# Mamba's step sizes laid out on 128 partitions of 160 columns instead of 32 of 544, and two durations in the schedule's model

## The chip, the core and the metric

One core of a Trainium2 chip runs the whole program in one launch. The metric is the time of one execution on the device, in microseconds (us). The core has five engines with a queue each: TensorE (PE in the profile, its weight loads apart as PEld), VectorE (DVE), ScalarE (ACT), GpSimd (POOL) and SyncE (SP), which here only issues DMAs. ACT issues a few DMAs too. An engine takes its instructions in the order of the program and waits where the next one is not ready.

## The reference

A two-layer streaming encoder over 512 prompt frames and 32 frames of a running stream, so 544 columns in the kernel. The first layer mixes with Mamba-2, the second with stick-breaking attention; both have half-step SwiGLU blocks before and after. The part that matters here, cut from the reference:

```python
zxbcdt = h @ w_in                                   # 1024 -> 5152, the last 32 are one step size per head
dt_raw = zxbcdt[..., D_INNER + CONV_DIM:]
xbc, conv_new = causal_dwconv(xbc, conv0, conv_w, conv_b)
xbc = silu(xbc)                                     # x, B and C of 4 groups of 8 heads
dt = softplus(dt_raw + dt_bias)
A = -exp(a_log)
# chunk by chunk, a = dt * A, x_c = x * dt:
a_cs = cumsum(a_c)
y_diag = einsum(C B, exp(a_cs_i - a_cs_j), x_c);  y_off = einsum(C, state) * exp(a_cs)
new_state = state * exp(a_cs[-1]) + einsum(B, exp(a_cs[-1] - a_cs), x_c)
y = (y + xs * d_skip) * silu(z);  grouped RMS norm;  out = y @ w_out
```

## The kernel before

Activations lie as 128 channels by 544 columns. A dense product is done in fp32 parts: weights and inputs are split into a high and a low part, and each 128-row chunk takes three products (high by high, high by low, low by high), each on two halves of 272 columns. The order prints them as three rows `mm<-xh,whi`, `mm<-xl,whi`, `mm<-xh,wlo`, each x2. Such three rows are called a triple below; a product of a 128-wide block of `w_in` has eight triples, and the products write two PSUM buffers (`mm`) in turn.

The Mamba stage (`mamba`, L938) cuts the 544 columns into four chunks of 128 (c = 0 to 3, the prompt) and one of 32 (c = 4, the running stream) and does the scan for four groups of eight heads, one after another (g = 0 to 3). For a chunk of a group there are

- the transposes of x (`aux<-ident,xs`) and of B (`aux<-ident,B`), and the product of C and B (`aux<-C,B`), in `turn_x`, `turn_b` and `decay`;
- the row `ab` of cumulated steps, broadcast to all partitions by an SP DMA from the DRAM copy `acs_d` (`load_ab`, L1139). There are two buffers `ab`, so a chunk's load waits for the output block of the chunk two before;
- on ACT the distances (`ex<-ab,tok`, 8 instructions), their exponential and that of `ab`; on DVE `ex<-ex,cb`; on POOL `ab<-ab,C` and the old state by its decay, `st<-st,fade`;
- the state product (`aux<-xw,btok`), and the output block (`output`, L1267): per pair of heads `aux<-ex,xd`, and for c > 0 `aux<-ab,st`. A block of c > 0 has 16 matmuls in the order, 8 for c = 0. Here it is called the output block of the chunk.

Step sizes come first (`steps`, L961). One dense block `dt` (unit 40 of `win`) gives 32 useful rows; its other 96 rows repeat other columns and are not read. On 32 partitions by 544 columns DVE does some twenty instructions for the softplus, then the scan `acs`; ACT writes `acs` to DRAM and makes `wend`; then, for each of the five chunks, PE transposes `acs`, `dt` and `wend` and DVE copies them to `tok`.

Between these pieces PE does the stage's dense products (`dense`), in the order of MSEQ (L40): inputs of a group (B, C, four x blocks), gates (z), outputs (o). Inputs go through `conv` (DVE, ACT, POOL), and a product waits for a free `mm` buffer, which its conv or gate frees, and for its split weights (`whi` by ACT or POOL, `wlo` by DVE).

The order on PE, DVE, ACT and POOL is not written out. `Plan` (L56) holds a model: each chain of work is a generator that yields steps `("T", duration, emit)` and the like ("T" is PE, "V" and "W" DVE, "S" ACT, "G" POOL), waits and slots. `Plan.run` (L137) always takes the step that can start first in the model, the lower rank on a tie, calls its emit, and moves the model's clock on by the duration given. The emitted order is then kept on the chip (`ordered`, L1396). So a duration in a `yield` changes the order of everything behind it, and nothing else. The dense chain has rank 50, after all others, and fills PE in the model.

Of the kernel before, what the change touches and what calls it, by code (L numbers as in the profile page):

```python
# [4 lines left out]
F32 = mybir.dt.float32  # L5
F32R = mybir.dt.float32r
BF16 = mybir.dt.bfloat16
AF = mybir.ActivationFunctionType
ALU = mybir.AluOpType

P = 128
# [159 lines left out]
def s_cost(n, psum=False):  # L171
    return n / 1200.0 + (0.052 if psum else 0.094)


def v_cost(n):
    return n / 960.0 + 0.069


def _body(tc, io):
# [22 lines left out]
    with ExitStack() as ctx:  # L202
# [3 lines left out]
        def halves(ap):  # L206
            return ap.rearrange("p (a b) -> p a b", a=2)
# [47 lines left out]
        convb = vecs[:, 96:120]  # L255
        ssmg = vecs[:, 120:136]
        dskip = vecs[:, 136:152]
        dtb = vecs[0:32, 152:153]
        alog = vecs[0:32, 153:154]
        hist = const.tile([P, 24, 3], F32, name="hist")  # L260
        nc.sync.dma_start(hist, io["hist"])

# [675 lines left out]
        def mamba(norm, after, ready, ahead):  # L938
            with tc.tile_pool(name="mt", bufs=1, reuse_waits="tile") as tmp, \
# [11 lines left out]
                chunks = [(c * P, P) for c in range(NCH)] + [(TP, TS)]  # L951
                tok = tmp.tile([P, 5, 96], F32, tag="tok", name="tok")
                cstate = tmp.tile([P, 24, 6], F32, tag="cstate", name="cstate")
                acs_d = pd.tile([32, T], F32, name="acs_d")
                acoef = const.tile([32, 1], F32, name="acoef")
                got = {}

                def hm(name, tag, bufs):
                    return tmp.tile([32, T], F32, tag=tag, name=name, bufs=bufs)

                def steps(ps):  # L961

                    cost = v_cost(T)
                    yield "wait", "r"
                    rv = halves(norm.r[:, :])
                    v = hm("dv", "ex", 2)
                    yield "W", cost, lambda: V.tensor_tensor(out=halves(v[:, :]), in0=ps[0:32, :, :H], in1=rv[0:32], op=ALU.mult)
                    yield "put", "mm"
                    yield "S", 0.15, lambda: S.activation(acoef, alog, AF.Exp), "exp"
                    yield "V", 0.08, lambda: V.tensor_scalar(acoef, acoef, -1.0, None, op0=ALU.mult)  # L970
                    yield "V", cost, lambda: V.tensor_scalar(v, v, dtb, None, op0=ALU.add)
                    e = hm("de", "ex", 2)
                    yield "V", cost, lambda: V.scalar_tensor_tensor(out=e, in0=v, scalar=-1.0, in1=v, op0=ALU.mult, op1=ALU.min)
                    yield "S", s_cost(T), lambda: S.activation(e, e, AF.Exp), "exp"
                    s = hm("ds", "xd", 2)
                    yield "V", cost, lambda: V.tensor_scalar(s, e, 2.0, None, op0=ALU.add)
                    yield "V", 3.5, lambda: V.reciprocal(s, s)
                    yield "V", cost, lambda: V.tensor_tensor(out=s, in0=s, in1=e, op=ALU.mult)
                    s2 = hm("dw", "xd", 2)
                    yield "V", cost, lambda: V.tensor_tensor(out=s2, in0=s, in1=s, op=ALU.mult)  # L980
                    q = hm("dq", "xw", 2)
                    yield "V", cost, lambda: V.tensor_scalar(q, s2, 1.0 / 17.0, None, op0=ALU.mult)
                    for k in (15, 13, 11, 9, 7, 5, 3):
                        yield "V", cost, lambda: V.scalar_tensor_tensor(out=q, in0=q, scalar=1.0 / k, in1=s2, op0=ALU.add, op1=ALU.mult)
                    yield "V", cost, lambda: V.scalar_tensor_tensor(out=q, in0=q, scalar=1.0, in1=s, op0=ALU.add, op1=ALU.mult)
                    yield "V", cost, lambda: V.tensor_scalar(q, q, 2.0, None, op0=ALU.mult)
                    dtt = hm("dt", "st", 3)
                    yield "V", cost, lambda: V.scalar_tensor_tensor(out=dtt, in0=v, scalar=0.0, in1=q, op0=ALU.max, op1=ALU.add)
                    a = hm("da", "xw", 2)
                    yield "V", cost, lambda: V.tensor_scalar(a, dtt, acoef, None, op0=ALU.mult)  # L990
                    keep = hm("keep", "ab", 2)

                    def starts():
                        G.memset(keep, 1.0)
                        for c in range(5):
                            G.memset(keep[:, c * P:c * P + 1], 0.0)
                    yield "G", 1.0, starts
                    acs = hm("acs", "st", 3)
                    yield "V", 2 * cost, lambda: V.tensor_tensor_scan(acs, keep, a, 0.0, ALU.mult, ALU.add)
                    nc.scalar.dma_start(acs_d, acs)  # L1000
                    wend = hm("wend", "st", 3)

                    def ends():
                        for o, n in chunks:
                            S.activation(wend[:, o:o + n], acs[:, o:o + n], AF.Exp, scale=-1.0, bias=acs[:, o + n - 1:o + n])
                    yield "S", 5 * s_cost(P), ends, "exp"
                    for c, (o, n) in enumerate(chunks):
                        yield "get", "aux"
                        pt = aux()

                        def turn():
                            for j, src in enumerate((acs, dtt, wend)):
                                TE.transpose(pt[:n, j * 32:(j + 1) * 32], src[:, o:o + n], ident[:32, :32])
                        yield "T", 0.3, turn
                        yield "W", v_cost(96), lambda: V.tensor_copy(tok[:n, c, :], pt[:n, 0:96])
                        yield "put", "aux"
                    yield "set", "tok"

                def scale():
# [119 lines left out]
                def load_ab(g, c):  # L1139
                    off, n = chunks[c]  # L1140
                    yield "wait", "tok", ("in", g, 4)
                    if g > 0:
                        yield "wait", ("ab", g - 1, 4)
                    yield "get", "ab"
                    ab = got["ab", g, c] = tmp.tile([P, 8, n], F32, tag="ab", name="ab", bufs=2)
                    nc.sync.dma_start(ab, acs_d[8 * g:8 * g + 8, off:off + n].partition_broadcast(P))
                    yield "sleep", 5.0
                    yield "set", ("ab", g, c)

# [117 lines left out]
                def output(g, c):  # L1267
                    off, n = chunks[c]
                    src = off if c < 4 else SOFF
                    xs = got["x", g]  # L1270
                    need = [("ex", g, c), ("xd", g, c), ("xw", g, c), ("cd", g, c)]
                    yield "wait", *need
                    if c > 0:
                        yield "wait", ("st", g, before(c))
                    if c == 0:
                        yield "get", "y"
                        got["y", g] = tmp.tile([P, 4, T], F32, tag="y", name="y", bufs=NY)
                        yield "set", ("y0", g)
                    else:
                        yield "wait", ("y0", g)  # L1280
                    yield "get", "aux"
                    py = aux()
                    xd, ex, ab = got["xd", g, c], got["ex", g, c], got["ab", g, c]

                    def emit(t):
                        for b in range(2):
                            h = 2 * t + b
                            dst = py[64 * b:64 * b + 64, t * P:t * P + n]
                            TE.matmul(dst, xd[:n, h, :], ex[:n, h, :], start=True, stop=c == 0)
                            if c > 0:  # L1290
                                TE.matmul(dst, got["st", g, before(c)][:, h, :], ab[:, h, :], start=False, stop=True)
                    for t in range(4):
                        yield "T", (0.24 if n < P else 0.52) if c else 0.25, lambda: emit(t)
                    yield "set", ("y", g, c)
                    yield "put", "ex"
                    yield "put", "xd"
                    yield "put", "ab"
                    pyv = py[:, :].rearrange("p (t i) -> p t i", t=4)[:, :, :n]
                    yv = got["y", g][:, :, off:off + n]

                    def skip(t):
                        V.scalar_tensor_tensor(out=yv[:, t], in0=xs[:, t, src:src + n], scalar=dskip[:, 4 * g + t:4 * g + t + 1], in1=pyv[:, t],
                                               op0=ALU.mult, op1=ALU.add)
                    for t in range(4):
                        yield "W", v_cost(n) + 0.06, lambda: skip(t)
                    yield "put", "aux"
                    yield "set", ("out", g, c)
# [789 lines left out]
```

## Time and profile before

| | |
|---|---|
| median of 3 runs | 2349.7 us (2348.56 to 2353.23) |
| the profiled execution | 2348.45 us |
| its span in the profile | 2346.7 us |
| PE busy | 2307.8 us, 98% |
| DVE busy | 1714.5 us, 73% |
| ACT busy | 1048.6 us, 45% |
| POOL busy | 592.2 us, 25% |
| mean granted TensorE clock | 0.988 of full |

The page counts an engine as busy while one of its instructions runs, so PE at 98% says how little it waits, not how fast it is: the clock that was granted stands apart (1.00 is 2.4 GHz, 0.50 is 1.2 GHz). Times in a row of the timeline are from the start of the span; what stands in brackets at its end is how long the engine sat idle before it, and what ended that.

### The profile page before, as it was taken

The numbers are of one execution on the slowest core, as the hardware profiler recorded it, in microseconds if no ns is written. First come the engines' busy times: TensorE is split into PE (matmuls) and PEld (weight loads), VectorE is DVE, ScalarE is ACT, GpSimd is POOL, SyncE is SP. The second block draws the span as 40 slices with busy tenths as digits, with TensorE's granted clock in tenths as the row PEclk, the third lists the DMA queues.
The fourth block names the chain that finished last, engine by engine and source line by source line (L and its number), as shares of the span: only waits on it lengthen the run. The fifth ranks groups of instructions, "written<-read, shape, count | busy, mean of one in ns | idle before, by whom it ended". The sixth has DMA issues, their size and how long they took to land.

```text
span 2346.7 us, 42561 instructions
## 1 busy us (share of the span) xinstructions
PE 2307.8 (98%) x17759; PEld 2216.6 (94%) x17766; DVE 1714.5 (73%) x2236; ACT 1048.6 (45%) x1530; POOL 592.2 (25%) x575
## 2 busy tenths in 40 slices
PE   9999999989999999999999999999999999999997
PEld 8999999979999999999999999999965799999997
DVE  7677786777877676777857767777678686777857
ACT  5333334477646353333345433333478553333343
POOL 3322122144323022221211122211333122122214
PEclk9999999999999999999999999999998999999999
DMA  5233323333333232333233333232211132333232
GB/s 158 78 104 104 95 67 91 106 89 102 100 101 88 82 118 78 103 104 95 66 106 94 115 100 91 90 108 67 87 41 32 37 117 74 107 91 104 64 104 75
DMA packets 112081, 213.17 MB, mean 91 GB/s; under 512 B 12528, under 2 KB 34544, under 8 KB 111888
## 3 DMA queue, kind: packets, MB, share of 16 engines
q1 hardware_dynamic: 109104, 204.92, 29.6%
q10 hardware_dynamic: 2784, 5.52, 0.7%
q8 instruction: 140, 2.29, 0.4%
q14 instruction: 53, 0.43, 0.1%
HBM read 204.83 MB, written 5.58 MB: 90 GB/s over the span
## 4 chain that ended last, share of the span: by engine, by line
PE 92%; DVE 4%; ACT 2%; DMA 1%; issue 1%; POOL 0%; SPq 0%; DVEq 0%; ACTq 0%; POOLq 0%
PE mm L191 81%; PE z L191 5%; PE aux L191 4%; PE f L191 1%; PE o L191 1%; DVE wlo L191 1%; DVE xl L191 1%; ACT whi L191 1%; DVE x L191 1%; DMA x<-in_x 0%; DMA wraw<-in_wpg 0%; DVE fu L191 0%; DVE sl L191 0%; ACT zt L191 0%; POOL ab L191 0%
## 5 line engine op out<-in xcount | busy, mean ns | idle before, releaser
L191 PE MATMUL mm<-xh,whi 128*128 128x272 f32 x2096 | 514.3, 293 | 1.1 <-ACT whi L191 0.5
L191 PE MATMUL mm<-xl,whi 128*128 128x272 f32 x2096 | 509.9, 291 | 2.5 <-DVE xl L191 2.5
L191 PE MATMUL mm<-xh,wlo 128*128 128x272 f32 x2096 | 508.4, 291 | 2.1 <-DVE wlo L191 2.1
L191 ACT ACTIVATE whi<-wraw 128x1024 fp32r<-128x1024 f32 (+3 forms) x220 | 189.1, 860 | 409.2 <-PE mm L191 284.3
L191 PEld LDWEIGHTS mm<-xh,whi 128*128 128x128 f32 x2096 | 360.1, 190 | 9.9 <-issue 7.8
L191 PEld LDWEIGHTS mm<-xh,wlo 128*128 128x128 f32 x2096 | 360.3, 190 | 2.9 <-DVE wlo L191 2.9
L191 PEld LDWEIGHTS mm<-xl,whi 128*128 128x128 f32 x2096 | 359.7, 190 | 3.6 <-DVE xl L191 3.5
L191 PE MATMUL mm<-xfh,whi 128*128 128x272 f32 x1152 | 332.0, 288 | 0.0
L191 PE MATMUL mm<-xfl,whi 128*128 128x272 f32 x1152 | 331.9, 288 | 0.0
L191 PE MATMUL mm<-xfh,wlo 128*128 128x272 f32 x1152 | 331.7, 288 | 0.0
L191 DVE TENSOR_TENSOR wlo<-wraw,whi 128x1024 fp32r<-128x1024 f32 (+3 forms) x253 | 257.5, 1018 | 71.1 <-ACT whi L191 56.1
L191 PE MATMUL mm<-hh,whi 128*128 128x272 f32 x1408 | 291.3, 288 | 0.0
L191 PE MATMUL mm<-hh,wlo 128*128 128x272 f32 x1408 | 291.0, 288 | 0.0
L191 PE MATMUL mm<-hl,whi 128*128 128x272 f32 x1408 | 290.7, 288 | 0.0
L191 ACT ACTIVATE whi<-a 128x1024 fp32r<-128x1024 f32 x126 | 133.8, 1062 | 311.0 <-PE mm L191 202.8
L191 DVE TENSOR_TENSOR wlo<-a,whi 128x1024 fp32r<-128x1024 f32 x144 | 176.5, 1225 | 102.2 <-ACT whi L191 68.9
L191 PEld LDWEIGHTS mm<-hl,whi 128*128 128x128 f32 x1408 | 221.2, 188 | 0.0
L191 PEld LDWEIGHTS mm<-hh,whi 128*128 128x128 f32 x1408 | 220.9, 188 | 0.0
L191 PEld LDWEIGHTS mm<-hh,wlo 128*128 128x128 f32 x1408 | 220.4, 188 | 0.2 <-DVE wlo L191 0.2
L191 PEld LDWEIGHTS mm<-xfh,wlo 128*128 128x128 f32 x1152 | 216.8, 188 | 0.0
L191 PEld LDWEIGHTS mm<-xfl,whi 128*128 128x128 f32 x1152 | 216.8, 188 | 0.0
L191 PEld LDWEIGHTS mm<-xfh,whi 128*128 128x128 f32 x1152 | 216.7, 188 | 0.0
(291 smaller groups left out, 4223.4 us busy)
## 6 DMA issues: line engine op xcount, KB each, us to landing
a<-in_wgu SPq DMA_DIRECT2D x144, 512.0 KB, 4.0
wraw<-in_wd SPq DMA_DIRECT2D x128, 256.0 KB, 2.7
wraw<-in_win SPq DMA_DIRECT2D x41, 512.0 KB, 3.7
wraw<-in_wgu SPq DMA_DIRECT2D x30, 512.0 KB, 3.6
wraw<-in_wd SPq DMA_DIRECT2D x32, 384.0 KB, 3.2
ab<-acs_d SPq DMA_DIRECT2D x16, 512.0 KB, 4.8
wraw<-in_wout SPq DMA_DIRECT2D x16, 512.0 KB, 3.7
wraw<-in_wpg SPq DMA_DIRECT2D x16, 512.0 KB, 3.6
```

The costliest lines, as they stand in the source:

```text
L191: ins = getattr(self.engine, op)(*args, **kw)
```

## The change

Five edits, all in the Mamba stage and its host-side layout:

- Unit 40 of `win` repeats the 32 step columns four times, so the product `dt` gives the same 32 rows on all four quarters of the partitions. Its shape stays.
- `steps` takes from quarter c the columns of chunk c, and from the first quarter chunk 4, in six DVE instructions, so the chain works on 128 partitions by 160 columns. Bias and `a_log` are repeated alike.
- `acs`, `dt` and `wend` are turned by three transposes of 128 by 128 and three of 32 by 32 in one piece instead of five pieces of three, and two DVE copies fill `tok` instead of five.
- `acs_d` has 128 rows of 160, and `load_ab` reads its eight rows from quarter c.
- In the model, one fourth of an output block is now 0.87 instead of 0.52 (c = 1 to 3), 1.2 instead of 0.24 (c = 4) and 0.44 instead of 0.25 (c = 0). The model's durations of the step chain follow its new shapes.

```diff
-        dtb = vecs[0:32, 152:153]
-        alog = vecs[0:32, 153:154]
+        dtb = vecs[:, 152:153]
+        alog = vecs[:, 153:154]
...
-                acs_d = pd.tile([32, T], F32, name="acs_d")
-                acoef = const.tile([32, 1], F32, name="acoef")
+                acs_d = pd.tile([P, P + TS], F32, name="acs_d")
+                acoef = const.tile([P, 1], F32, name="acoef")
...
-                    return tmp.tile([32, T], F32, tag=tag, name=name, bufs=bufs)
+                    return tmp.tile([P, P + TS], F32, tag=tag, name=name, bufs=bufs)
...
-                    rv = halves(norm.r[:, :])
                     v = hm("dv", "ex", 2)
-                    yield "W", cost, lambda: V.tensor_tensor(out=halves(v[:, :]), in0=ps[0:32, :, :H], in1=rv[0:32], op=ALU.mult)
+
+                    def pieces():
+                        V.memset(v[:, P:], 0.0)
+                        for c, (o, n) in enumerate(chunks):
+                            rows = slice(32 * (c % 4), 32 * (c % 4) + 32)
+                            at = 0 if c < 4 else P
+                            while n:
+                                a, b = divmod(o, H)
+                                m = min(n, H - b)
+                                V.tensor_tensor(out=v[rows, at:at + m], in0=ps[rows, a, b:b + m], in1=norm.r[rows, o:o + m], op=ALU.mult)
+                                o, n, at = o + m, n - m, at + m
+                    yield "W", 0.1 + 5 * v_cost(P) + 0.1, pieces
...
-                    yield "V", 3.5, lambda: V.reciprocal(s, s)
+                    yield "V", 1.1, lambda: V.reciprocal(s, s)
...
-                        for c in range(5):
-                            G.memset(keep[:, c * P:c * P + 1], 0.0)
-                    yield "G", 1.0, starts
+                        for c in (0, P):
+                            G.memset(keep[:, c:c + 1], 0.0)
+                    yield "G", 0.4, starts
...
-                        for o, n in chunks:
+                        for o, n in ((0, P), (P, TS)):
                             S.activation(wend[:, o:o + n], acs[:, o:o + n], AF.Exp, scale=-1.0, bias=acs[:, o + n - 1:o + n])
-                    yield "S", 5 * s_cost(P), ends, "exp"
-                    for c, (o, n) in enumerate(chunks):
-                        yield "get", "aux"
-                        pt = aux()
-
-                        def turn():
-                            for j, src in enumerate((acs, dtt, wend)):
-                                TE.transpose(pt[:n, j * 32:(j + 1) * 32], src[:, o:o + n], ident[:32, :32])
-                        yield "T", 0.3, turn
-                        yield "W", v_cost(96), lambda: V.tensor_copy(tok[:n, c, :], pt[:n, 0:96])
-                        yield "put", "aux"
+                    yield "S", 2 * s_cost(P), ends, "exp"
+                    yield "get", "aux"
+                    pt = aux()
+
+                    def turn():
+                        for j, src in enumerate((acs, dtt, wend)):
+                            TE.transpose(pt[:, j * P:(j + 1) * P], src[:, :P], ident)
+                            TE.transpose(pt[:TS, 384 + j * 32:416 + j * 32], src[:32, P:], ident[:32, :32])
+                    yield "T", 0.6, turn
+
+                    def turned():
+                        V.tensor_copy(tok[:, 0:4, :].rearrange("p c (j h) -> p c j h", j=3), pt[:, 0:384].rearrange("p (j c h) -> p c j h", j=3, c=4))
+                        V.tensor_copy(tok[:TS, 4, :], pt[:TS, 384:480])
+                    yield "W", v_cost(384) + v_cost(96), turned
+                    yield "put", "aux"
...
-                    nc.sync.dma_start(ab, acs_d[8 * g:8 * g + 8, off:off + n].partition_broadcast(P))
+                    rows, at = (32 * c + 8 * g, 0) if c < 4 else (8 * g, P)
+                    nc.sync.dma_start(ab, acs_d[rows:rows + 8, at:at + n].partition_broadcast(P))
...
-                        yield "T", (0.24 if n < P else 0.52) if c else 0.25, lambda: emit(t)
+                        yield "T", (1.2 if n < P else 0.87) if c else 0.44, lambda: emit(t)
...
-    col = np.zeros((P, 2), np.float32)
-    col[:32, 0] = g["ssm_dt_bias"][0]
-    col[:32, 1] = g["ssm_a_log"][0]
+    col = np.tile(np.stack([g["ssm_dt_bias"][0], g["ssm_a_log"][0]], axis=1), (4, 1))
...
-    a["win"] = np.concatenate([units(win[:, :5120]), units(np.concatenate([win[:, 5120:], win[:, 5024:5120]], axis=1))], axis=0)
+    a["win"] = np.concatenate([units(win[:, :5120]), units(np.tile(win[:, 5120:], (1, 4)))], axis=0)
```

What PE does around the turning of the step sizes, before (the first of five such pieces and the start of the second; `acs`, `dt`, `wend` are the step chain's results):

```order
L191 MATMUL aux<-ident,acs 128x32
L191 MATMUL aux<-ident,dt 128x32
L191 MATMUL aux<-ident,wend 128x32
L191 MATMUL mm<-xh_4016,whi 128x272 x2
L191 MATMUL mm<-xl_4017,whi 128x272 x2
L191 MATMUL mm<-xh_4016,wlo 128x272 x2
L191 MATMUL mm<-xh_4047,whi 128x272 x2
L191 MATMUL mm<-xl_4048,whi 128x272 x2
L191 MATMUL mm<-xh_4047,wlo 128x272 x2
L191 MATMUL aux<-ident,acs 128x32
```

And in the change, where the whole turning is one piece:

```order
L191 MATMUL aux<-ident,acs 128x128
L191 MATMUL aux<-ident,acs 32x32
L191 MATMUL aux<-ident,dt 128x128
L191 MATMUL aux<-ident,dt 32x32
L191 MATMUL aux<-ident,wend 128x128
L191 MATMUL aux<-ident,wend 32x32
L191 MATMUL mm<-xh_4289,whi 128x272 x2
```

Between the norm's product at the start of the stage (`aux<-acc,ones`) and the first turning stand 83 triples before and 65 in the change, so the scan of the first group begins 18 triples earlier.

PE in the first group's scan, from the last matmul of the output block of chunk 2 to the first of chunk 3, before:

```order
L191 MATMUL aux<-ab,st 64x128
L191 MATMUL aux<-xw,btok 128x512
L191 MATMUL aux<-ident,xs 32x128 x4
L191 MATMUL aux<-ident,B 32x128
L191 MATMUL aux<-C,B 32x32
L191 MATMUL aux<-ex,xd 64x128
```

And in the change, from the same matmul on:

```order
L191 MATMUL aux<-ab,st 64x128
L191 MATMUL aux<-xw,btok 128x512
L191 MATMUL mm<-xh_4189,whi 128x272 x2
L191 MATMUL mm<-xl_4190,whi 128x272 x2
L191 MATMUL mm<-xh_4189,wlo 128x272 x2
L191 MATMUL mm<-xh_4240,whi 128x272 x2
L191 MATMUL mm<-xl_4241,whi 128x272 x2
L191 MATMUL mm<-xh_4240,wlo 128x272 x2
L191 MATMUL aux<-ident,xs 32x128 x4
L191 MATMUL aux<-ident,B 32x128
```

After these stand two more triples, `aux<-C,B`, two triples, and then the output block of chunk 3. Before, no triple stands between the output blocks of chunks 2, 3 and 4 of the first group; now six and two do (and between chunks 1 and 2 five, where two stood).

PE at the border of the second and the third group, before: the end of the second group's output block of chunk 4, behind which 18 triples come ahead of the next scan piece.

```order
L191 MATMUL aux<-ex,xd 64x32
L191 MATMUL aux<-ab,st 64x32
L191 MATMUL mm<-xh_4329,whi 128x272 x2
L191 MATMUL mm<-xl_4330,whi 128x272 x2
L191 MATMUL mm<-xh_4329,wlo 128x272 x2
```

In the change the third group's first output block (`aux<-ex,xd 64x128 x8`) follows two triples behind it:

```order
L191 MATMUL aux<-ab,st 64x32
L191 MATMUL aux<-xw,btok 128x512
L191 MATMUL mm<-xh_4289,whi 128x272 x2
L191 MATMUL mm<-xl_4290,whi 128x272 x2
L191 MATMUL mm<-xh_4289,wlo 128x272 x2
L191 MATMUL aux<-ident,xs 128x128 x4
L191 MATMUL aux<-ident,B 128x128
L191 MATMUL mm<-xh_4329,whi 128x272 x2
L191 MATMUL mm<-xl_4330,whi 128x272 x2
L191 MATMUL mm<-xh_4329,wlo 128x272 x2
L191 MATMUL aux<-ex,xd 64x128 x8
L191 MATMUL aux<-C,B 128x128
```

On ACT the same place reads, in the change (`out_ssm_s<-st` writes the second group's last state out; `ex`, `ab` behind it are the third group's chunk 0):

```order
L191 ACTIVATE ex<-ex 32x256
L191 ACTIVATE ab<-ab 128x256
L1277 DMA out_ssm_s<-st 128x512
L191 ACTIVATE ex<-ab,tok 128x128 x8
L191 ACTIVATE ex<-ex 128x1024
L191 ACTIVATE ab<-ab 128x1024
```

Before, convolution work of the third group stands behind that DMA, and the third group's distances come later.

The triples between output blocks in the four groups (from the end of one to the start of the next, c = 0 to 1, 1 to 2, 2 to 3, 3 to 4) are, before: 20, 2, 0, 0; 8, 14, 6, 7; 18, 9, 4, 7; 17, 9, 5, 18. In the change: 15, 5, 6, 2; 13, 8, 2, 6; 16, 6, 4, 12; 19, 4, 18, 0.

## Rows read from the trace of the kernel before

**Rows 1.** The page, part 1: busy us, share of the span, instructions.

```profile
PE 2307.8 (98%) x17759; PEld 2216.6 (94%) x17766; DVE 1714.5 (73%) x2236; ACT 1048.6 (45%) x1530; POOL 592.2 (25%) x575
```

**Rows 2.** Windows: length, busy by engine, granted clock (third last), DMA share, GB/s.

```profile
391.00:840.00 449.00, 440.36 (x3526) 416.17 (x3525) 334.14 (x567) 253.44 (x408) 139.77 (x174) 0.97 0.34 97
501.71:523.40 21.69, 13.05 (x91) 9.23 (x89) 16.19 (x35) 14.73 (x28) 12.40 (x12) 0.76 0.23 68
506.40:509.82 3.42, 3.42 (x24) 2.58 (x21) 2.82 (x6) 1.02 (x2) 1.90 (x3) 0.50 0.00 0
513.23:520.06 6.83, 3.55 (x30) 3.18 (x31) 2.96 (x7) 5.46 (x13) 4.34 (x3) 0.50 0.06 22
...
584.91:588.32 3.41, 3.41 (x17) 3.41 (x16) 2.73 (x6) 1.33 (x2) 0.00 (x0) 0.50 0.76 169
```

**Rows 3.** Timeline of PE, first group's chunks 2 to 4: start, duration, [idle before].

```profile
503.38 0.49 PE L191 MATMUL aux<-C,B 128*128 128x128 f32 x2 [1.40 <-DVE xd L191]
...
505.73 0.32 PE L191 MATMUL aux<-ab,st 128*64 128x128 f32 x1 [1.50 <-POOL ab L191]
...
515.35 0.66 PE L191 MATMUL aux<-ex,xd 128*64 128x128 f32 x2 [4.24 <-DVE xd L191]
517.17 0.48 PE L191 MATMUL aux<-ab,st 128*64 128x128 f32 x1 [1.16 <-POOL ab L191]
...
523.04 0.27 PE L191 MATMUL aux<-ex,xd 32*64 32x32 f32 x2 [0.35 <-DVE xd L191]
```

**Rows 4.** Timeline of ACT in the same stretch: what it waited for.

```profile
508.28 0.66 ACT L191 ACTIVATE xs<-cv 128x547 f32<-128x547 f32 x1 [1.52 <-DVE cv L191]
```

**Rows 5.** Timeline of PE: starts of pairs of rows that give a pitch.

```profile
454.29 0.41 PE L191 MATMUL mm<-xh,wlo 128*128 128x272 f32 x2
...
455.29 0.41 PE L191 MATMUL mm<-xl,whi 128*128 128x272 f32 x2
...
461.92 0.41 PE L191 MATMUL mm<-xh,wlo 128*128 128x272 f32 x2
...
463.20 0.42 PE L191 MATMUL mm<-xl,whi 128*128 128x272 f32 x2
...
466.82 0.41 PE L191 MATMUL mm<-xh,whi 128*128 128x272 f32 x2
...
469.83 0.41 PE L191 MATMUL mm<-xh,whi 128*128 128x272 f32 x2
...
496.86 0.45 PE L191 MATMUL aux<-ex,xd 128*64 128x128 f32 x4
...
498.81 1.13 PE L191 MATMUL aux<-xw,btok 128*128 128x512 f32 x2
...
500.02 0.41 PE L191 MATMUL mm<-xl,whi 128*128 128x272 f32 x2
...
580.16 0.30 PE L191 MATMUL aux<-ex,xd 32*64 32x32 f32 x2
...
583.59 0.30 PE L191 MATMUL aux<-ab,st 128*64 128x32 f32 x2
```

**Rows 6.** Timeline of SP, POOL and PE, third group: chunk 3 behind chunk 1.

```profile
632.88 0.38 SPq L1146 DMA_DIRECT2D ab<-acs_d  x1
644.29 2.36 POOL L191 TENSOR_TENSOR ab<-ab,C 128x1024 f32<-128x1024 f32 x1 [1.70 <-DVE fade L191]
648.25 0.45 PE L191 MATMUL aux<-ex,xd 128*64 128x128 f32 x4
```

**Rows 7.** Timeline of DVE: the step chain.

```profile
411.23 3.53 DVE L191 RECIPROCAL ds<-ds 32x544 f32<-32x544 f32 x1
...
446.73 0.71 DVE L191 SCALAR_TENSOR_TENSOR dt<-dv,dq 32x544 f32<-32x544 f32 x1
```

**Rows 8.** Timeline of POOL, first group: one operation at two places.

```profile
463.58 1.04 POOL L191 TENSOR_TENSOR xw<-xd,tok 128x512 f32<-128x512 f32 x1 [19.23 <-DVE xd L191]
...
494.85 2.04 POOL L191 TENSOR_TENSOR xw<-xd,tok 128x512 f32<-128x512 f32 x1
```

More of the change, by code (lines that the diff above doesn't have):

```diff
@@ L953, in mamba @@
                 cstate = tmp.tile([P, 24, 6], F32, tag="cstate", name="cstate")
-                acs_d = pd.tile([32, T], F32, name="acs_d")
-                acoef = const.tile([32, 1], F32, name="acoef")
+                acs_d = pd.tile([P, P + TS], F32, name="acs_d")
+                acoef = const.tile([P, 1], F32, name="acoef")
                 got = {}
                 def hm(name, tag, bufs):
-                    return tmp.tile([32, T], F32, tag=tag, name=name, bufs=bufs)
+                    return tmp.tile([P, P + TS], F32, tag=tag, name=name, bufs=bufs)
                 def steps(ps):
-                    cost = v_cost(T)
+                    cost = v_cost(P + TS)
                     yield "wait", "r"
-                    rv = halves(norm.r[:, :])
                     v = hm("dv", "ex", 2)
-                    yield "W", cost, lambda: V.tensor_tensor(out=halves(v[:, :]), in0=ps[0:32, :, :H], in1=rv[0:32], op=ALU.mult)
+                    def pieces():
[9 more added lines that the diff above has]
+                    yield "W", 0.1 + 5 * v_cost(P) + 0.1, pieces
                     yield "put", "mm"
@@ L973, in steps @@
                     yield "V", cost, lambda: V.scalar_tensor_tensor(out=e, in0=v, scalar=-1.0, in1=v, op0=ALU.mult, op1=ALU.min)
-                    yield "S", s_cost(T), lambda: S.activation(e, e, AF.Exp), "exp"
+                    yield "S", s_cost(P + TS), lambda: S.activation(e, e, AF.Exp), "exp"
                     s = hm("ds", "xd", 2)
                     yield "V", cost, lambda: V.tensor_scalar(s, e, 2.0, None, op0=ALU.add)
-                    yield "V", 3.5, lambda: V.reciprocal(s, s)
+                    yield "V", 1.1, lambda: V.reciprocal(s, s)
                     yield "V", cost, lambda: V.tensor_tensor(out=s, in0=s, in1=e, op=ALU.mult)
```

## Prediction

> **What bounds the kernel now.** I read the page's busy times first: PE is busy 2307.8 us of the span [rows 1], so only what PE does, waits for, or does at a lower clock counts, and other engines matter where they make it wait. Then the windows, with the Mamba stage apart: 449.00 us with PE busy 440.36, so 8.64 us idle, at a mean granted clock of 0.97 [rows 2]. A second window shows where: 501.71 to 523.40 has 21.69 us with PE busy 13.05, again 8.64. All the idle time of the stage lies in the first group's chunks 2, 3 and 4. The timeline of PE there gives five waits: 1.40 on DVE's xd, 1.50 on POOL's ab, 4.24 and 1.16 on the same two a chunk later, and 0.35 [rows 3], together 8.65.
>
> Why PE waits there is read from the order and from ACT. Between these output blocks PE has two, none and none triples to do, so it stands as soon as a chunk's inputs are late. They are late because `ab` and `ex` go through ACT, and ACT stood 1.52 us for a convolution that DVE had not finished [rows 4]: the convolutions of the second group share the engines with the scan, and no dense product comes, since both `mm` buffers wait for just these convolutions.
>
> The clock: it is granted at 0.50 (1.2 GHz) in two stretches of that place, one with PE busy 3.42 us, one with 3.55 [rows 2]. Before them PE had waited. There is another kind: at 584.91 the clock falls for 3.41 us though PE is busy throughout, right behind the output block of chunk 4 that ends at 583.59 with its small matmuls [rows 2, 5]. The windows show this one; the stage has four, one behind each group's chunk 4.
>
> **The change part by part.**
>
> *The step chain.* Twelve DVE instructions like the one of 0.71 us [rows 7] and five cheaper ones go from 544 to 160 columns, the reciprocal of 3.53 by the same ratio to some 1.0; six short ones and a memset replace the first multiplication. I estimate 17 us of DVE before and 8 after. PE waits for nothing of this now: all idle time of the stage is elsewhere [rows 2, 3]. So I cost it at nothing. Its cover is the dense products ahead of the turning, 65 triples of 0.753 us (four take 3.01, rows 466.82 and 469.83 [rows 5]). The change draws on that cover: the turning stands 18 triples, 13.6 us, earlier. If the chain is late there, PE waits for `wend`; its last parts (scan, table load, two exponentials) I put some 0.8 us ahead of PE. From a loss of 1 us to nothing; I take nothing, because DVE gets lighter.
>
> *The turning.* From 454.29 to 455.29 is 1.00 us for two rows that take 0.50 at the pitch above, so three narrow transposes cost 0.50; five such pieces 2.5. The new piece has six. The nearest rows are the four wide transposes, one of B and one product: 461.92 to 463.20 less 0.50, so 0.78 [rows 5]. I take 0.8: a gain of 1.7; from 1.0 to 2.0.
>
> *The first group's scan.* Now 15, 5, 6 and 2 triples stand between its output blocks. Is that enough? The longest chain is from the end of a block, which frees `ab`, to the block two chunks on: load, distances, two exponentials, POOL's product. In the third group of the trace it runs from 632.88 to 644.29 + 2.36 = 646.65, so 13.8 us, and PE starts that block at 648.25 [rows 6] without a wait. In the change, PE has between the end of chunk 1's block and chunk 3's: 11 triples (8.3), one block (496.86 to 498.81, so 1.95 [rows 5]), two state products (at most 1.13 each, the row at 498.81; I take 0.9) and transposes of 1.3: 13.4 us. So chunk 3 comes about 0.4 us late, and I add 0.5 for each of chunks 2 and 4. The 8.65 us of waits goes, 1.4 comes: and with the long waits the two low stretches that follow them, worth half of 3.42 + 3.55, so 3.5 us. The four stretches behind chunk 4 I leave as they are.
>
> The Trainium skill, in "TensorE: Matmul & The Clock Gate" under "HAM oscillation", says that the clock falls when TensorE has stood idle too long between bursts. By that rule the stretches behind chunk 4 would not exist, and a schedule without idle time would gain their 4 x 1.7 us too. The row at 584.91 shows a fall with PE busy for all of it, so the trace does not agree, and the sum leaves that out.
>
> *The other groups.* The model now holds a block of c > 0 at 4 x 0.87 = 3.48 us, and it takes 1.95; chunk 4 at 4.8, and it takes 3.66 (580.16 to 583.59 and the last row's 0.30 [rows 5]); before it held 2.08 and 0.96. So where the model was too quick for PE it is now too slow: PE reaches the next piece earlier than planned, by 1.5 us for each wide block, and waits for inputs that were ordered just in time. The counted triples show it. Second group, chunk 1 to 3: 10 triples, a block, two state products, transposes, 12.6 us against 13.8, so 1.2 of wait; chunk 4, 8 triples between, 1 us (nothing at best, 2.8 if its chain is as long as chunk 3's). Border to the third group: only two triples lie between chunk 4's block and the next group's first, and on ACT that group's distances stand behind the output DMA of the old state. From the DMA on, distances, exponential and DVE's product follow one another, and behind that `xd` and POOL's `xw` for the next state product. I put 1 us of wait on the block and 1 on the state product. Third group, chunk 1 to 3, with 10 triples and a norm's product: 13.1 against 13.8, so 0.7. Fourth: 0.5, since 18 triples stand ahead of chunk 3. Together 5.4, and with the border a further low stretch, 1.7.
>
> POOL decides how far this is right: `xw` takes 1.04 us at one place and 2.04 at another, beside DVE's work [rows 8]. With the longer value in each of these six chains the waits grow by 6 us; with the shorter and slack elsewhere they can vanish. The Trainium skill explains it, in "SBUF — State Buffer" under "Who interferes with whom": the two engines share a port pair that one of them holds for a whole instruction. The trace agrees (2.04 for 1.04); by the page alone no wait can be placed.
>
> *The rest.* `acs_d` is written once and read in the same amounts; the loads keep their size. Six instructions in place of one hold the `dt` buffer some 1 us longer at the stage's start; the next product into it stands about 1 us behind. Nothing, up to 0.5 lost.
>
> **The sum**, against the profiled execution of 2348.45 us: 8.65 + 3.5 + 1.7 = 13.85 gained; 1.4 + 5.4 + 1.7 = 8.5 given back; 5.4 less, so 2343.1. The median of the runs is 2349.7, 1.25 above that execution; half of this I put on: 2343.6 us.
>
> **Rivals.**
>
> 1. *The scan is simply filled.* The new waits stay at 2 us and no low stretch is added: 13.85 - 2 = 11.9 less, 2337.5. For it: three of four groups run without a wait now with as few as 4 to 9 triples between blocks. Against: these had a model that made PE late, not early.
>
> 2. *The stall moves.* First group filled, but what PE gains there it stands elsewhere: waits of 10 and two more stretches (3.4) cancel the 13.85: 2348.5 to 2350. For it: the lead of 1.5 us a block is systematic, the gain is one place.
>
> 3. *The model leads PE too far.* Twelve wide blocks at 1.5 us and four of chunk 4 at 1.1 make 22.6 us of waits if no slack takes any up, and with waits in each of three groups three more low stretches come, 5.1. Then 13.85 - 27.7, so 14 us slower, 2362. It decides from the point where all that is new passes 13.85; at a middling 20 it is 2355. Against: the model's triple is 0.705 us (`t_cost`) and takes 0.753, which gives back 13 us over the 273 triples between the first output block and the last, and much dense work stands at most places.
>
> 4. *The change does not do what it says*: the durations are called measured, and 0.87 is not what the row of 1.95 for four gives. That is the ground of 2 and 3 and has no chance of its own.
>
> **How the numbers follow.** The forecast (about 3 to 9 us less) 0.47, rival 1 0.22, rival 2 0.20, rival 3 0.11. A measurement of this kernel can tell about 0.2% from no change, 4.7 us. Rival 1 and three quarters of the forecast lie below 2345.0, so faster 0.57; the rest of the forecast and most of rival 2 within, 0.31; rival 3 and a little of 2 above 2354.4, 0.12. The range takes in the forecast and rivals 1 and 2: 2336 to 2352. The likeliest case by itself is 2340 to 2347.
>
> **What would show it.** Right: in the first group's scan no wait of PE over 1 us, and the clock at 1.00 until chunk 4's block has ended; one low stretch still behind most chunk 4 blocks; small waits before output blocks and state products of the second and third groups, the largest at their border; the stage some 5 us shorter. The step chain's DVE rows near 0.3 us. Wrong: the first group still waits several us at chunk 2 or 3; a wait for `wend` at the turning; waits of over 10 us in groups two to four; or low stretches scattered over the stage with PE busy.

## The result, and the profile after

The changed kernel takes 2337.44 us (median of 4 runs, 2335.02 to 2337.85), the kernel before 2349.13 beside it: ratio 0.995, interval 0.9938 to 0.9963, 11.7 us faster. The forecast was 2343.6, with a range of 2336 to 2352. So sign and range held, and the gain was twice the forecast; the experiments show that one of the change's two halves made a larger gain, and that the other half took a part of it away.

The page of the change, part 1 (answers to [rows 1]; the profiled execution took 2335.02 us, its span 2332.9):

```profile
PE 2295.5 (98%) x17750; PEld 2206.8 (95%) x17757; DVE 1707.0 (73%) x2237; ACT 1045.5 (45%) x1528; POOL 599.3 (26%) x570
```

I compare the stage between the start of its first and of its last norm product (`aux<-acc,ones`), which leaves out dense work at its ends that has no wait. Windows of the kernel before: length, busy by engine, granted clock third last.

```profile
391.10:793.59 402.49, 393.85 (x3156) 369.70 (x3155) 299.02 (x524) 232.03 (x378) 129.23 (x167) 0.97 0.34 97
```

The same of the change, with the stretches at half clock, and (585.10) the second group's block of chunk 4 for contrast:

```profile
389.43:783.85 394.42, 389.82 (x3147) 366.52 (x3146) 290.86 (x525) 229.16 (x376) 134.63 (x162) 0.98 0.34 99
498.04:501.46 3.42, 3.42 (x18) 3.42 (x17) 2.27 (x6) 2.35 (x4) 0.00 (x0) 0.50 0.52 158
585.10:588.50 3.40, 3.40 (x31) 2.82 (x30) 1.09 (x3) 1.60 (x6) 1.60 (x2) 1.00 0.22 82
641.40:644.82 3.42, 3.42 (x17) 3.24 (x17) 1.42 (x5) 0.00 (x0) 0.00 (x0) 0.50 0.43 132
750.63:757.46 6.83, 6.83 (x34) 6.57 (x33) 3.56 (x9) 1.32 (x2) 0.00 (x0) 0.50 0.10 38
```

The stage is 8.07 us shorter. Half of that is idle time: 402.49 - 393.85 = 8.64 before, 394.42 - 389.82 = 4.60 now. The other half, 4.03, is PE's busy time, at 0.50 for 13.67 us now where it was for 23.91 before, 20.63 of them with PE busy (six windows; three of them in [rows 2]).

All waits of PE in the stage, in the timeline (start, duration, idle before and who ended it); compare [rows 3]:

```profile
489.83 0.69 PE L191 MATMUL aux<-xw,btok 32*128 32x512 f32 x1 [0.90 <-POOL xw L191]
...
493.75 0.24 PE L191 MATMUL aux<-ab,st 128*64 128x32 f32 x1 [0.86 <-POOL ab L191]
...
592.60 0.33 PE L191 MATMUL aux<-ex,xd 128*64 128x128 f32 x2 [0.64 <-DVE y L191]
...
594.62 0.70 PE L191 MATMUL aux<-xw,btok 128*128 128x512 f32 x1 [0.51 <-POOL xw L191]
...
615.56 0.35 PE L191 MATMUL aux<-C,B 128*128 128x128 f32 x1 [0.46 <-DVE fade L191]
...
629.53 0.66 PE L191 MATMUL aux<-xw,btok 32*128 32x512 f32 x1 [0.80 <-DVE btok L191]
...
748.11 0.30 PE L191 MATMUL aux<-ab,st 128*64 128x32 f32 x2 [0.30 <-POOL ab L191]
```

Two stand in the first group, two at the border to the third, two in the third, one in the fourth: no wait over 1 us, 4.47 together.

The turning, in PE's timeline, and on ACT the exponentials that it needs:

```profile
438.51 0.62 ACT L191 ACTIVATE wend<-acs 128x128 f32<-128x128 f32 x2
```

```profile
439.32 0.40 PE L191 MATMUL aux<-ident,acs 128*128 128x128 f32 x2
439.66 0.46 PE L191 MATMUL aux<-ident,dt 128*128 128x128 f32 x2
440.05 0.46 PE L191 MATMUL aux<-ident,wend 128*128 128x128 f32 x2
440.44 0.52 PE L191 MATMUL mm<-xh,whi 128*128 128x272 f32 x2
```

`wend` is there at 439.13, 0.9 us ahead of its transpose, and six transposes take 1.12 us. The step chain on DVE (answers to [rows 7]):

```profile
408.41 1.15 DVE L191 RECIPROCAL ds<-ds 128x160 f32<-128x160 f32 x1
...
428.18 0.32 DVE L191 SCALAR_TENSOR_TENSOR dt<-dv,dq 128x160 f32<-128x160 f32 x1
```

Outside the stage 5.7 us of the profiles' difference of 13.8 remain: 1.7 ahead of it, and 4.0 in the attention stage (1667.05 to 1907.29 before), where PE runs the same instructions in the same order:

```profile
1667.05:1907.29 240.24, 230.69 (x1293) 169.38 (x1299) 180.96 (x279) 158.69 (x274) 75.48 (x83) 0.97 0.19 57
```

```profile
1657.36:1893.56 236.20, 225.84 (x1294) 166.18 (x1299) 181.12 (x279) 158.53 (x274) 75.84 (x83) 1.00 0.19 58
```

The idle time there is 9.55 before and 10.36 after; what differs is the clock (0.97, 1.00).

### The profile page after: what moved, and what is told of

It reads as the page before. It is cut to its first block, busy times and chain, and to the rows that moved or that the text cites. A ratio compares the mean times of both kernels' runs of the same rounds, so it can differ in the third digit from the quotient of the medians.

```text
span 2332.9 us, 42534 instructions
## 1 busy us (share of the span) xinstructions
PE 2295.5 (98%) x17750; PEld 2206.8 (95%) x17757; DVE 1707.0 (73%) x2237; ACT 1045.5 (45%) x1528; POOL 599.3 (26%) x570
## 4 chain that ended last, share of the span: by engine, by line
PE 89%; DVE 5%; ACT 2%; issue 2%; POOL 1%; DMA 1%; SPq 0%; DVEq 0%; ACTq 0%; POOLq 0%
PE mm L191 80%; PE z L191 5%; PE aux L191 2%; PE f L191 1%; DVE wlo L191 1%; PE o L191 1%; POOL ab L191 1%; DVE xl L191 1%; ACT whi L191 1%; DVE x L191 1%; DMA x<-in_x 0%; DVE sl L191 0%; DMA wraw<-in_wpg 0%; DVE fu L191 0%; POOL st L191 0%
```

## The experiments

The question was which half of the change, the layout or the durations, made the gain, and by what. Theory A: the scan's place in the plan, which follows from the length that the planner gives the step chain. Theory B: the durations, or the work saved.

All results in one table. "Stage" is the window above, "idle" its length less PE's busy time, "low" the time in it at a granted clock of 0.50, each of the profiled execution.

| kernel | median us (runs) | ratio to before, interval | stage | idle | low |
|---|---|---|---|---|---|
| before, first profile | 2349.13 (4) | | 402.49 | 8.64 | 23.9 |
| before, second profile | 2356.13 (1) | | 411.91 | 9.12 | 44.4 |
| the change | 2337.44 (4) | 0.9938 to 0.9963 | 394.42 | 4.60 | 13.7 |
| the change again | 2338.11 (5) | 0.9939 to 0.9965 | 394.45 | 4.66 | 13.7 |
| durations alone | 2355.57 (11) | 1.0013 to 1.0031 | 413.38 | 10.31 | 44.4 |
| layout alone | 2330.49 (6) | 0.991 to 0.9936 | 386.89 | 0.90 | 6.8 |
| layout alone again | 2332.10 (6) | 0.9904 to 0.9933 | 386.86 | 0.90 | 6.8 |
| layout, measured durations | 2341.99 (5) | 0.9953 to 0.9977 | 396.52 | 5.07 | 20.5 |
| layout, chunk 4's duration | 2336.12 (5) | 0.9927 to 0.9955 | 391.66 | 2.76 | 13.6 |
| layout, wide blocks' duration | 2340.44 (5) | 0.9946 to 0.9976 | 395.21 | 3.54 | 20.5 |
| layout, near durations | 2334.40 (5) | 0.9916 to 0.9944 | 390.36 | 0.87 | 13.7 |
| layout, shorter durations | 2339.36 (5) | 0.9937 to 0.9966 | 398.26 | 4.18 | 23.9 |
| layout, old chain costs | 2348.05 (11) | 0.9982 to 1.0 | 399.68 | 5.88 | 27.3 |
| before, short chain costs | 2338.84 (6) | 0.9934 to 0.9962 | 392.61 | 3.55 | 10.2 |

**Durations alone.** The kernel before with all three durations of the change:

```
-  yield "T", (0.24 if n < P else 0.52) if c else 0.25, lambda: emit(t)
+  yield "T", (1.2 if n < P else 0.87) if c else 0.44, lambda: emit(t)
```

> The kernel before with only the three durations of the output block changed (1.2, 0.87 and 0.44); the step sizes stay on 32 partitions. In its order the first group's output blocks have 20, 2, 0 and 0 triples between them, as before. Theory A (the moved turning and the lighter step chain fill the first group's scan, the durations only redistribute triples among the later groups and cost small waits there): the five waits of 8.65 us stay, some 0 to 5 us of new waits come in groups two to four; 2348 to 2354 us. Theory B (the durations fill the scan): the first group's waits shrink to under 3 us and the time falls to 2340 to 2343 us.

Slower, by 0.13 to 0.31%: theory A, a little above its range. The first group keeps its waits (PE's timeline, two of them), PE's idle time is 1.2 to 1.7 us more than in the two profiles of the kernel before, and a long stretch at half clock follows (windows):

```profile
512.46 0.40 PE L191 MATMUL aux<-ex,xd 128*64 128x128 f32 x2 [4.26 <-DVE xd L191]
514.27 0.48 PE L191 MATMUL aux<-ab,st 128*64 128x128 f32 x1 [1.42 <-POOL ab L191]
```

```profile
389.14:802.52 413.38, 403.07 (x3156) 376.66 (x3155) 297.01 (x522) 238.49 (x385) 140.91 (x165) 0.95 0.34 94
513.11:533.59 20.48, 18.84 (x90) 14.46 (x91) 8.51 (x21) 10.05 (x25) 6.25 (x7) 0.50 0.27 78
```

The kernel before has such a long stretch in its second profile too (below), so it need not come from the durations. What makes up the rest of the 6.6 us between the medians is not shown.

**Layout alone.** The changed kernel with the line above set back to 0.24, 0.52 and 0.25.

> The changed kernel with the old durations of the output block (0.24, 0.52 and 0.25): the layout alone. In its order the first group's output blocks have 22, 7, 17 and 2 triples between them, groups two to four 20, 8, 13, 8; 16, 6, 7, 12; 17, 9, 5, 18. Theory A: the first group runs with less than 2 us of waits and the later groups wait for nothing or little, because more triples stand between the blocks than in the change; 2334 to 2338 us, as fast as the change or up to 3 us faster. Theory B (the durations make the gain): the waits of the first group are still over 5 us and the time is 2344 to 2349 us.

2330.49, faster than A expected, and 7.6 less than the change beside it on the same chip (2338.11). The stage in windows, with the only stretch at half clock:

```profile
389.54:776.43 386.89, 385.99 (x3148) 363.25 (x3147) 291.98 (x527) 232.62 (x377) 123.94 (x163) 0.99 0.35 101
645.24:652.06 6.82, 6.82 (x34) 6.50 (x33) 4.15 (x9) 0.66 (x1) 0.00 (x0) 0.50 0.30 93
```

Against the change the stage is 7.53 us shorter: 3.70 idle and 3.83 busy, and half of the 6.85 us of low clock that is gone is 3.4. So the layout makes the whole gain, and the durations cost on either layout. This version beats both kernels.

**Layout with measured durations.** `(0.91 if n < P else 0.49) if c else 0.27`.

> The changed kernel with the durations that the trace gives for an output block: a quarter of 1.95 us (0.49), of 3.66 us (0.91) and for the first chunk 0.27. Triples between the blocks: 18, 6, 10, 7; 26, 8, 8, 4; 14, 11, 5, 2; 17, 9, 5, 9. Theory A: within 2 us of the layout alone, 2334 to 2338 us, since the first group is filled in both and the later groups keep 4 triples or more nearly everywhere. A rival, that long durations are what helps because they keep PE from being late: between the change and the kernel before, 2339 to 2345 us.

Theory A missed: 2341.99, slower than the change. One wait makes most of the idle time, in PE's timeline and on DVE, which frees the `mm` buffer:

```profile
580.57 0.49 PE L191 MATMUL mm<-xh,whi 128*128 128x272 f32 x2 [3.76 <-DVE zt L191]
```

```profile
579.72 0.70 DVE L191 TENSOR_TENSOR zt<-mm,r 128x544 f32<-128x544 f32 x1
```

No output block waits there: in the new order `zt` stands on DVE behind `wlo` and the scan's `xd`, `btok` and `cb`. Truer numbers did not make a better plan.

**Which duration costs.** Chunk 4's alone (`(1.2 if n < P else 0.52) if c else 0.25`) and the wide blocks' alone (`(0.24 if n < P else 0.87) if c else 0.44`):

> The changed kernel with the old duration for the wide blocks (0.52 and 0.25) and the new one for chunk 4 (1.2). Triples between the blocks: 22, 7, 17, 2; 23, 12, 6, 8; 12, 6, 15, 5; 17, 9, 5, 18. Theory A1: the first group waits for nothing, the others for under 1 us, 2329 to 2333 us. Theory A2: 2336 to 2340 us.

> The changed kernel with the old duration for chunk 4 alone (0.24 in place of 1.2); the wide blocks stay at 0.87 and 0.44. Triples between the blocks: 15, 5, 6, 2; 11, 9, 6, 9; 20, 7, 4, 1; 19, 4, 18, 0. Theory A1 (the wide blocks' duration of 0.87 gives back what the layout gains): the first group waits some 1.8 us as in the change, 2336 to 2340 us. Theory A2 (chunk 4's duration of 1.2 does it, by the border of the second and third groups): 2330 to 2333 us.

2336.12 and 2340.44: each costs without the other, so A1 and A2 both fail as explanations of the whole. The layout alone did not run on this chip; the kernel before took 2349.64 on it, and 2349.01 beside the layout alone (2330.49), so for chunk 4's duration, whose interval overlaps with that of the layout alone, the cost is the less certain one. The two costs do not add up to that of both, 7.6. With chunk 4's alone the largest wait, 1.99 us, is again one that the triples between blocks did not show, for ACT's `xs`:

```profile
517.78 0.48 PE L191 MATMUL aux<-ident,xs 128*128 128x128 f32 x1 [1.99 <-ACT xs L191]
```

**Layout with near, and with shorter durations.** `(0.24 if n < P else 0.49) if c else 0.27` and `(0.24 if n < P else 0.2) if c else 0.1`:

> The layout alone with the wide block's durations set to the measured ones and chunk 4's kept at 0.24: 0.49 for 0.52 and 0.27 for 0.25, a change of some 0.1 us for a block. Triples between the blocks: 18, 6, 10, 7; 28, 14, 12, 2; 16, 6, 17, 7; 17, 9, 5, 9. If the accuracy of these numbers is what matters, it is at most 1 us from the layout alone, 2329 to 2332 us. If the plan turns on small differences (three of four groups get another order), a wait of several us can come from another place, as the 3.76 us for an `mm` buffer with the measured durations: 2334 to 2343 us.

> The layout alone with durations of the output block below the measured ones (0.2, chunk 4 0.24, first chunk 0.1). Triples between the blocks: 22, 10, 11, 5; 17, 14, 14, 9; 14, 10, 8, 18; 24, 12, 11, 4: nowhere under 4, where the layout alone has a 2 in the first group. If the number of triples between blocks decides, this is as fast as the layout alone or up to 2 us faster, with under 1 us of waits: 2328 to 2332 us. If a duration below the measured one makes the plan wrong as one above it does, new waits of 2 to 6 us come: 2334 to 2342 us.

2334.40 and 2339.36. The near durations, 0.03 us a quarter away, cost 2.3 us against the layout alone on the same chip (2332.10; the runs of the two overlap, 2333.96 to 2336.34 and 2330.62 to 2334.49), and 3.5 in the stage, without any more waiting (idle 0.87): low clock alone, 13.7 for 6.8. For the shorter ones the second expectation held. And 4 or more triples between all blocks did not help: that kernel waits for `xs`, `yh`, `yl` and `zt` instead. The number of triples between output blocks orders these kernels badly.

**The chain's cost in the plan.** The layout alone, its short instructions planned at the old costs:

```
-  cost = v_cost(P + TS)
+  cost = v_cost(T)
-  yield "V", 1.1, lambda: V.reciprocal(s, s)
+  yield "V", 3.5, lambda: V.reciprocal(s, s)
...
```

> The layout alone (old durations of the output block), but the planner is told the old costs of the step chain (instructions of 544 columns, a reciprocal of 3.5 us): the instructions are the short ones, only their places are planned as if they were long. In its order 112 triples stand ahead of the first output block where the layout alone has 93 and the kernel before 119, and 19, 10, 0 and 0 between the blocks of the first group. Theory A (the gain comes from the place that the planner gives the scan, since it sees a shorter chain): chunks 3 and 4 of the first group wait again, 4 to 9 us in sum, with low stretches behind the waits; 2341 to 2349 us. Theory B (the gain is the work itself: fewer transposes, a lighter DVE): no wait over 1 us, within 3 us of the layout alone, 2329 to 2334 us.

And the kernel before with its long instructions planned at the short costs, much the same lines the other way round:

> The kernel before (32 partitions, its own durations of the output block), where only the planner is told the short costs of the step chain; the instructions stay the long ones. From the first group's chunk 2 on its order has the same triples between the output blocks as the layout alone (7, 17, 2; 20, 8, 13, 8; and so on), with 98 ahead of the first block and 17 behind it. Theory A (the planner's view of the chain is what counts, the work itself little): the first group runs with under 2 us of waits at its output blocks; PE pays 1.7 us for the narrow transposes and 0 to 6 us where it waits for the late chain at the turning; 2332 to 2339 us. Theory B (the chain must really be short): PE waits over 8 us at the turning, for `acs` or `wend`, low stretches follow, 2343 to 2352 us.

These two decide. With the chain in fact short, but planned long, the gain is gone: 2348.05, with 2349.64 for the kernel before beside it, and the first group waits again, at chunks 3 and 4, 4.96 us in all (PE's timeline, chunk 3):

```profile
507.61 0.25 PE L191 MATMUL aux<-C,B 128*32 128x32 f32 x2 [1.88 <-DVE xd L191]
509.97 0.32 PE L191 MATMUL aux<-ab,st 128*64 128x128 f32 x1 [1.61 <-POOL ab L191]
```

With the chain in fact long, but planned short, most of it is there: 2338.84. PE pays at the turning (timeline), and behind the wait with low clock (windows):

```profile
443.00 0.24 PE L191 MATMUL aux<-ident,wend 32*128 32x32 f32 x1 [2.48 <-ACT wend L191]
```

```profile
389.79:782.40 392.61, 389.06 (x3157) 365.42 (x3156) 299.64 (x524) 233.75 (x380) 126.97 (x166) 0.99 0.35 99
444.04:450.86 6.82, 6.82 (x32) 6.04 (x31) 2.53 (x5) 3.00 (x3) 0.00 (x0) 0.50 0.80 228
```

The first group's output blocks wait for nothing there. Of the stage's 15.60 us between the kernel before (its first profile) and the layout alone, 9.88 then come from the plan, and the short instructions are worth the other 5.72: no wait for `wend`, no low clock behind it, fewer transposes. The medians of one chip say the same, 2351.63 for the kernel before, 2338.84 and 2332.10: 12.8 and 6.7. The shares depend on which is changed first: from the kernel before by way of the short chain planned long, the stage gives 2.81 to the instructions and 12.79 to the plan. By either way the plan has the larger part.

**The kernels once more.** No edit.

> The changed kernel once more, for a second profile. If the attention stage's shorter time (4.05 us less in the profile of the change, with no low clock there, where the profile before has two stretches of 6.83 us) is part of the change, it shows no low clock in that stage again. If it is a matter of the execution, low stretches can stand there in this profile, or be missing in the profiles of the other kernels of this call, whose attention stage has the same instructions. The waits of PE in the first Mamba stage should be the same to 0.5 us in sum (4.5), the time 2335 to 2338 us.

> The kernel before once more, for a second profile: the same five waits, 8.6 us within 0.3, at the same places, and seven units of low clock in the stage. If the two low stretches of the attention stage belong to this kernel's place in time they stand there again, and the stage takes 240.2 us; if they are a matter of the execution they can be elsewhere or missing, and the stage takes 236.2 us.

> The layout alone once more, for a second profile beside the others of this call: waits of the stage 0.9 us within 0.4, the time within 2329 to 2334 us; the low stretches of the attention stage may be elsewhere or missing.

The waits came back at the same places, in sum to 0.5 us, in all three, and the stage of the change and of the layout alone to 0.03 us. That of the kernel before did not: with 9.12 us idle for 8.64 it took 9.4 us more, with 20.5 us more at half clock (the expectation's seven units are the 23.9 us of its first profile). Half of this is one stretch behind the same waits, 20.48 us where the first profile has 6.83 and 3.42. The other half stands in or behind chunk 4's block of the other groups, with PE busy throughout: 6.8 us each for 3.4 (windows):

```profile
391.03:802.94 411.91, 402.79 (x3156) 377.60 (x3155) 298.93 (x524) 232.08 (x378) 128.84 (x167) 0.95 0.33 95
516.22:536.70 20.48, 19.00 (x92) 14.84 (x93) 9.19 (x22) 9.67 (x25) 5.96 (x6) 0.50 0.28 79
587.90:594.72 6.82, 6.82 (x33) 6.50 (x34) 3.89 (x8) 1.61 (x2) 0.00 (x0) 0.50 0.44 91
666.40:673.23 6.83, 6.83 (x33) 6.66 (x33) 5.17 (x12) 1.90 (x2) 1.06 (x4) 0.50 0.51 136
775.63:782.46 6.83, 6.83 (x33) 6.51 (x34) 4.65 (x10) 0.66 (x1) 0.65 (x1) 0.50 0.21 73
```

And its attention stage took 238.82 instead of 240.24:

```profile
1676.42:1915.24 238.82, 228.74 (x1300) 167.57 (x1299) 180.99 (x279) 158.54 (x274) 75.54 (x83) 0.99 0.19 58
```

So the attention stage can differ between executions of one kernel, here by 1.4 us. The two profiles of the change have 236.2 and 236.3 there, those of the layout alone 239.7 both; the durations alone and the shorter durations have 236.2, the rest 238.8 to 240.3. What sets it was not found, and that it goes with the kernel as a whole is not excluded.

## Why the prediction was right, and where it was off

*What bounds the kernel* held: nearly all that the stage gained or lost is a wait of PE or a stretch at half clock; the turning's transposes are the rest that was found.

*The step chain, costed at nothing,* is the step that failed. As work it was sized well: DVE's busy time in the stage fell by 8.2 us (9 estimated), the cover held by 0.9 us (0.8), and nothing waits for `wend`. But the length that the planner gives it also sets where the scan starts, and the plan is worth most of the layout's gain: planned long, the same instructions give 2348.05, planned short 2330.49. The turning comes 18 triples earlier, the first output block 26 (93 triples ahead of it in the layout alone for 119 before, 112 when planned long). That the gain works through this place is read from the orders; the runs change the plan as a whole. The prediction counted the result (15, 5, 6, 2 triples) and did not see which edit had made it; so it could not see that the layout by itself leaves 22, 7, 17 and 2.

*The turning:* 1.12 us and not 0.8, a gain of 1.4 and not 1.7.

*The first group's scan:* the five waits went as said. 1.76 came for 1.4, but both waits stand at chunk 4, where 0.5 was forecast, and none at chunks 2 and 3, where 0.9 was: the sum is near by luck. Both are for POOL (`xw`, `ab`), which the prediction had named as the uncertain engine. DVE worked beside both rows of [rows 8], though: beside the 1.04 us on `btok`, `cb` and `cu`, which read `aux` or `mm`, beside the 2.04 us on `wlo` and `cv` (494.46 to 497.46), which read neither.

*The other groups, 5.4:* mis-sized, it is 2.71 (0.64, 0.51, 0.46, 0.80, 0.30). The border came out at 1.15 for 2 and the third group at 1.26 for 0.7; the second group, put at 2.2, waits for nothing. That the old model was too quick for PE is so for chunk 4 alone (0.96, and the rows named give 3.73 and not 3.66); the wide block stood at 2.08 for 1.95.

*The clock:* the added low stretch at the border (1.7) did not come, and low clock stands in or behind three blocks of chunk 4 (498.04, 641.40, 750.63, the last for twice as long), not four. The clock was at 1.00 until the first group's chunk 4 had ended, as forecast.

Made up for the stage: the waits give 4.04 (forecast 8.65 - 6.8 = 1.85), PE's busy time 4.03 (forecast 3.5 + 1.7 - 1.7 = 3.5): 8.07 for 5.4. Of the 4.03, the clock gave about 3.5 (half of 20.63 - 13.67) where the prediction's two terms make 1.8; with the turning's 1.4 that is 0.9 more than was measured, and where PE's other busy time grew was not found. The rest of the median's 11.7 is outside the stage, or lies in how often the kernel before runs with more low clock; the runs show that both vary, and not how much of either is in the median.

*The rivals.* Rival 1's time (2337.5) is the measured one, in part by luck: it takes its 11.9 us from the stage, which gave 8.07 in the profiles, and its waits of 2 us are 4.5; that no low stretch is added came true. Rivals 3 and 4 had it right that the durations are not the measured ones and cost time, 7.5 us of stage on the new layout, not 22. But accuracy is not the cure, since the measured ones cost more.

Open: why single numbers of the plan, near 0.5 us, move the time by 2 to 11 us can be told for each order (a wait for `zt`, `xs`, `yl`), but nothing here foretells it.

## What to carry to other kernels

Where a planner orders the work, an edit acts by what it does to the plan as much as by the work it saves: run the old instructions with the new costs and the new instructions with the old ones before giving either the credit. A duration in such a model is a tuning number; test it by itself, since a truer one can be slower (2341.99 for 2330.49 here). Change one half at a time: here one half was worth some 19 us and the other took back 7.6.

## What the runs showed of the hardware

Nearly equal waits go with different amounts of low clock: in two executions of the kernel before, 8.64 and 9.12 us of idle time went with 23.9 and 44.4 us at half clock, and the stage with 402.49 and 411.91 us. Only half of the difference lies behind those waits. Its runs, 2344.2 to 2356.1 us, spread as widely as the change gains (11.7 us), so one run of each kernel would not size such a gain.

The small matmuls of chunk 4's block go with a fall of the clock in some groups and not in others, with PE busy in both: 641.40 to 644.82 at 0.50 (the block runs from 638.26 to 642.25), 585.10 to 588.50 at 1.00 (the block from 585.12 to 588.85), in one trace. The layout alone has it in one group of four (645.24, 87 us behind PE's last wait, of 0.18 us), the kernel before in all four. In the second profile of the change the third group's stretch stands elsewhere: at 631.43 to 634.85, ahead of that block (from 639.90) and behind a wait of 0.83 us (629.64). What decides is not shown. By the Trainium skill, "TensorE: Matmul & The Clock Gate", "HAM oscillation", idle gaps are what brings the clock down; the stretches behind waits agree with that in kind (444.04 behind the wait of 2.48 us, which is shorter than the gap that the page names), the stretch at 645.24 does not.
